# Weight buffers at two fixed remainders of 256 bytes in place of rotating ones, in a float32 decoder trunk

## The chip, the cores and the metric

The kernel runs on one core of one Trainium2 chip. The metric is the device time of one execution in microseconds (us), as a median over runs. Five engines work on a core: TensorE (PE; its weight loads are listed as PEld), VectorE (DVE), ScalarE (ACT), GpSimd (POOL) and SyncE (SP, which here issues the weight transfers). SBUF is the memory on the chip that they read; each of its 128 partitions holds its own bytes, and "address" below means the byte within a partition. PSUM holds what TensorE accumulates.

## The reference

The input is one sequence of 256 positions with 2048 features. Two layers follow. Each has a token mixer (layer 0 a gated linear recurrence, HGRN2; layer 1 a gated MLP with a spatial gate) and a gated feed-forward block with a causal convolution of width 3 and 5632 hidden features. Cut to what matters here:

```python
for layer in range(2):
    mixed = hgrn2_mixer(h, ...) if layer == 0 else chunked_gmlp(h, ...)
    h = layer_norm(ALPHA * h + mixed, ln1_g[layer], ln1_b[layer])
    up = h @ w_up                        # 2048 x 11264
    a, b = jnp.split(up, 2, axis=-1)
    a = causal_conv3(a) + conv_b
    h = layer_norm(ALPHA * h + (silu(a) * b) @ w_down, ln2_g[layer], ln2_b[layer])
# mixers: x @ w_in (2048 x 8192, or 2048 x 4096), the mixing itself, and @ w_out (2048 x 2048)
```

Everything is float32. Nearly all of the work is in the products with the weight matrices, and the activations are only 256 rows, so each weight is used for two tiles of 128 rows and then dropped.

## The kernel before

**Split operands.** A product of float32 numbers is made out of three products of shorter ones. Every operand is split into a high part (the value cast to the type fp32r) and a low part (the value less its high part). For activations, `X` holds the input of a mixer or of the feed-forward block and `Y` the input of the second product; both have the shape 128 x 16 x 2 x 256: 16 tiles k of 128 features, each with 256 high and then 256 low values (2048 bytes). The product is high x high + high x low + low x high.

**Weights.** They come in chunks of 512 features by 512 columns (`raw`, 128 x 4 x 512, 1 MB each). `fetch` (L73) issues the transfer on SP; `convert` (L83) makes the high part `whi` on ScalarE (L95) and the low part `wlo` on VectorE (L96), in two halves of 128 x 1024 each. The pool `wp` has three buffers for each of `raw`, `whi` and `wlo`, and chunks take them in turn. `chunk` keeps three chunks ahead of the one in use (`AHEAD = 3`). The order of the chunks is a list that `want` fills (`plan_hgrn`, `plan_gmlp`, `plan_ffn`). Six chunks of the program go to an extra pool `xp` instead.

**Two forms of product.** In `block_b` (L152) the weights are stationary and `X` streams through. For each k and each 128 columns j it issues two matmuls into the same PSUM tile: `rest` (L168) with the low weights loaded and 256 high values of `X` streamed, and `both` (L161) with the high weights loaded and all 512 values of `X` streamed. So long and short matmuls alternate, each with a weight load of 128 x 128 of its own, and a chunk has 16 of each. Where `halves` is set (one block for each feed-forward block), the long ones are in part cut into pieces of 256. In `block_a` (L112) the activations are stationary and 512 weight columns stream: three matmuls for each k and half t of the rows, L125 (high activations, high weights), L126 (high, low) and L127 (low, high); a chunk has 24. `staggered_pass` (L675 to L677) does the same for the last part of one product.

**Where the buffers lie.** Pools lay their tiles one behind the other, and tiles without a use (`pad0`, `pady`, `pad1`, `gap`) fill up between them. In the built program of before `X` starts at address 16,640, a multiple of 256; each of its tiles is a multiple of 1024 bytes, so every operand taken from it starts at remainder 0 of 256. `Y` starts at 49,600, remainder 192. `whi` and `wlo` have 16 floats (`SKEW`) more than they need, so their size is 8256 bytes, 64 more than a multiple of 256: the three `whi` start at remainders 0, 64 and 128 (126,720, 134,976, 143,232), and so do the three `wlo` (151,552, 159,808, 168,064), with `gap` between the two groups. A chunk's high and low buffers have the same remainder. The slices within a buffer are multiples of 512 bytes and don't change it. Chunk after chunk the buffers turn through the remainders in the order 0, 128, 64. The buffers of the extra pool start at remainder 224, both halves.

Of the kernel before, what the change touches and what calls it, by code (L numbers as in the profile page):

```python
# [9 lines left out]
F32R = mybir.dt.float32r  # L10
# [5 lines left out]
P = 128  # L16
# [9 lines left out]
NB = 512  # L26
CK = 4
# [2 lines left out]
FFN_GROUPS = (3, 4, 4)  # L30
AHEAD = 3
LINE = 256
PAD_Y = 192
PAD1 = 160
SKEW = 16
BLOCK = {1: 32, 4: 32, 16: 64}
XSEQ = ((0, 2, 4), (2, 2, 0), (4, 4, 1), (8, 4, 1), (12, 4, 0))
TURN_ACT = 3
# [2 lines left out]
class Trunk:  # L41
# [4 lines left out]
    def __init__(self, ctx, tc, a):  # L46
# [11 lines left out]
        self.X = cp.tile([P, NK, 2, S], F32R, name="X")  # L58
        cp.tile([P, PAD_Y], mybir.dt.uint8, name="pady")
        self.Y = cp.tile([P, NK, 2, S], F32R, name="Y")  # L60
        self.z = cp.tile([P, 2, D], F32, name="z")
        cp.tile([P, PAD1], mybir.dt.uint8, name="pad1")
        self.small = ent(tc.tile_pool(name="small", bufs=2))
# [19 lines left out]
    def convert(self, raw, extra, pieces=2):  # L83
        nc = self.nc
        pool = self.xp if extra else self.wp
        size = CK * NB + (0 if extra else SKEW)
        hi = pool.tile([P, size], F32R, tag="hi", name="whi")
        if not extra:
            pool.tile([P, LINE - 3 * 4 * SKEW], mybir.dt.uint8, tag="gap", name="gap", bufs=1)
        lo = pool.tile([P, size], F32R, tag="lo", name="wlo")  # L90
        hi, lo = (x[:, : CK * NB].rearrange("p (k n) -> p k n", k=CK) for x in (hi, lo))
        n = CK // pieces
        for i in range(0, CK, n):
            s = slice(i, i + n)
            nc.scalar.copy(hi[:, s, :], raw[:, s, :])  # L95
            self.last_lo = nc.vector.tensor_tensor(  # L96
                lo[:, s, :], raw[:, s, :], hi[:, s, :].bitcast(F32), ALU.subtract
            )
        self.ready.append((hi, lo))
# [800 lines left out]
```

## Time and profile before

| | before |
|---|---|
| median of 3 runs | 2296.53 us (2296.07 to 2297.42) |
| the profiled execution's own time | 2296.34 us |
| its span, from the first to the last instruction | 2294.6 us |
| mean granted TensorE clock | 0.998 |
| DMA | 430.14 MB, mean 187 GB/s |
| instructions in the span | 31751 |

Times in the profile come from the profiled execution. A row of a group of instructions gives line, engine, operation, output<-inputs with shapes, and behind the count (x) the busy time in us, the mean length of one in ns and the engine's idle time just before them. A matmul's record lasts from its start until its results are drained, and the next one starts long before that, so the lengths of records of neighbouring matmuls overlap, and a row's busy time counts overlapping time once. What a matmul costs in a dense stream is its spacing: the time from its start to the next one's start. A row of a stretch of time gives from:to in us, the length, TensorE's busy time with the number of instructions that touch the stretch, the granted clock, the DMA share and GB/s. A row of the timeline gives start in us, length in us, engine, line and operation.

### The profile page before, as it was taken

How to read it: one execution, taken by the hardware profiler on the slowest of the kernel's cores; microseconds unless marked ns; L12 is line 12 of the kernel's file. 1: busy time of each engine (PE TensorE's matmuls, PEld its weight loads, DVE VectorE, ACT ScalarE, POOL GpSimd, SP SyncE). 2: the span in 40 equal slices, each digit the busy share in tenths (PEclk: the TensorE clock that was granted, in tenths of full speed). 3: DMA queues.
4: the chain of work that ended last, by engine and by line, in shares of the span. 5: the costliest groups of instructions: out<-in, count | busy, mean ns of one | idle time of the engine just before them, and what ended most of it. 6: DMA issues, size and time to landing. Idle time of an engine off the chain costs nothing.

```text
span 2294.6 us, 31751 instructions
## 1 busy us (share of the span) xinstructions
PE 2272.9 (99%) x12781; PEld 1930.8 (84%) x12781; DVE 1473.2 (64%) x2327; ACT 1104.6 (48%) x1698; POOL 48.5 (2%) x102
## 2 busy tenths in 40 slices
PE   8999999999999999999999999999999999999998
PEld 7888888888888888888888888888888888888886
DVE  5767677667765665556656676566765666465655
ACT  5656565545443444344444554454543444344542
POOL 3000000000000000000000000000000000000000
PEclk9999999999999999999999999999999999999999
DMA  7454545645565555555555675655575555555563
GB/s 259 150 183 144 191 148 163 217 164 189 188 233 184 184 183 195 191 183 186 189 193 172 213 218 184 223 180 174 179 239 181 187 189 192 186 184 189 178 202 111
DMA packets 214052, 430.14 MB, mean 187 GB/s; under 512 B 7544, under 2 KB 8336, under 8 KB 213904
## 3 DMA queue, kind: packets, MB, share of 16 engines
q1 hardware_dynamic: 209536, 415.26, 54.4%
q0 software_dynamic: 4368, 12.85, 1.9%
q8 instruction: 100, 1.64, 0.3%
q14 instruction: 48, 0.39, 0.0%
HBM read 425.98 MB, written 2.10 MB: 187 GB/s over the span
## 4 chain that ended last, share of the span: by engine, by line
PE 97%; DVE 1%; ACT 1%; DMA 1%; SPq 0%; issue 0%; DVEq 0%; ACTq 0%
PE pb L161 38%; PE pb L168 20%; PE pa L125 12%; PE pa L127 12%; PE pa L126 12%; PE pl L552 1%; DMA z<-in_x_dram 1%; DVE wlo L96 0%; PE pt L307 0%; PE pg L754 0%; PE pa L677 0%; PE pa L675 0%; PE pa L676 0%; PE po L524 0%; PE pout L644 0%; ACT whi L95 0%
## 5 line engine op out<-in xcount | busy, mean ns | idle before, releaser
L96 DVE TENSOR_TENSOR wlo<-raw,whi 128x1024 fp32r<-128x1024 f32 (+1 forms) x786 | 930.0, 1218 | 704.9 <-ACT whi L95 696.6
L161 PE MATMUL pb<-X,whi 128*128 128x512 f32 (+1 forms) x3960 | 1344.3, 390 | 1.9 <-DVE X L319 1.9
L95 ACT CAST whi<-raw 128x1024 fp32r<-128x1024 f32 (+1 forms) x786 | 789.4, 1046 | 908.6 <-PE pb L161 426.0
L168 PE MATMUL pb<-X,wlo 128*128 128x256 f32 x3840 | 1055.8, 283 | 0.0
L161 PEld LDWEIGHTS pb<-X,whi 128*128 128x128 f32 x3960 | 725.6, 188 | 164.5 <-DVE X L319 2.4
L168 PEld LDWEIGHTS pb<-X,wlo 128*128 128x128 f32 x3840 | 714.8, 188 | 6.5
L125 PE MATMUL pa<-whi,Y 128*128 128x512 f32 x928 | 366.2, 395 | 0.0
L127 PE MATMUL pa<-whi,Y 128*128 128x512 f32 x928 | 365.8, 394 | 0.0
L126 PE MATMUL pa<-wlo,Y 128*128 128x512 f32 x928 | 365.0, 393 | 0.0
L127 PEld LDWEIGHTS pa<-whi,Y 128*128 128x128 f32 x928 | 174.6, 188 | 40.6
L126 PEld LDWEIGHTS pa<-wlo,Y 128*128 128x128 f32 x928 | 174.5, 188 | 40.5
L125 PEld LDWEIGHTS pa<-whi,Y 128*128 128x128 f32 x928 | 174.6, 188 | 39.0
L206 ACT COPY rest<-pb 128x256 f32<-128x256 f32 x240 | 87.8, 369 | 114.0 <-PE pb L161 105.8
L125 PE MATMUL pa<-whi,X 128*128 128x512 f32 x256 | 101.0, 394 | 0.0
L127 PE MATMUL pa<-whi,X 128*128 128x512 f32 x256 | 100.6, 393 | 0.0
L126 PE MATMUL pa<-wlo,X 128*128 128x512 f32 x256 | 100.3, 392 | 0.0
L805 DVE SCALAR_TENSOR_TENSOR act<-a,cols,act 128x254 f32<-128x254 f32 (+1 forms) x176 | 73.0, 475 | 0.0
L127 PEld LDWEIGHTS pa<-whi,X 128*128 128x128 f32 x256 | 48.1, 188 | 11.0
L126 PEld LDWEIGHTS pa<-wlo,X 128*128 128x128 f32 x256 | 48.1, 188 | 10.7
L125 PEld LDWEIGHTS pa<-whi,X 128*128 128x128 f32 x256 | 48.1, 188 | 10.3
L399 DVE TENSOR_TENSOR z<-z,pa 128x512 f32<-128x512 f32 x40 | 27.3, 683 | 36.1 <-PE pa L127 31.7
L809 ACT ACTIVATE act<-act 128x256 f32<-128x256 f32 x88 | 33.8, 415 | 7.8 <-DVE act L805 7.6
(164 smaller groups left out, 1030.2 us busy)
## 6 DMA issues: line engine op xcount, KB each, us to landing
raw<-in_ffn_w_up_dram SPq DMA_DIRECT2D x176, 1024.0 KB, 4.9
raw<-in_ffn_w_down_dram SPq DMA_DIRECT2D x88, 1024.0 KB, 4.9
raw<-in_hg_w_in_dram SPq DMA_DIRECT2D x63, 1024.0 KB, 5.1
raw<-in_sg_w_in_dram SPq DMA_DIRECT2D x32, 1024.0 KB, 5.3
raw<-in_hg_w_out_dram SPq DMA_DIRECT2D x16, 1024.0 KB, 4.9
raw<-in_sg_w_out_dram SPq DMA_DIRECT2D x16, 1024.0 KB, 4.9
g<-in_ln_g_dram POOLq DMA_DIRECT2D x16, 256.0 KB, 6.3
b<-in_ln_b_dram POOLq DMA_DIRECT2D x16, 256.0 KB, 8.5
```

The source lines that it names most:

```text
L95: nc.scalar.copy(hi[:, s, :], raw[:, s, :])
L96: self.last_lo = nc.vector.tensor_tensor(lo[:, s, :], raw[:, s, :], hi[:, s, :].bitcast(F32), ALU.subtract)
L125: nc.tensor.matmul(ps[t], xh, hi[:, kk, :], start=n[t] == 0, stop=False)
L126: nc.tensor.matmul(ps[t], xh, lo[:, kk, :], start=False, stop=False)
L127: nc.tensor.matmul(ps[t], xl, hi[:, kk, :], start=False, stop=last)
L161: nc.tensor.matmul(ps[j][:, :, s], ch[0][:, k % CK, c], act[:, k, :, s], start=start and k == 0, stop=k == last, skip_group_check=halves,)
L168: nc.tensor.matmul(ps[j][:, 1, :], ch[1][:, k % CK, c], act[:, k, 0, :], start=False, stop=False, skip_group_check=halves,)
L206: nc.scalar.copy(r, ps[:, 1, :])
L399: nc.vector.tensor_tensor(zz, zz, ps, ALU.add)
L552: nc.tensor.matmul(ps[n * j : n * j + n, th, :], K[:, own(th, n, j)], moving(th, j), start=True, stop=True, tile_position=(0, n * j),)
L805: nc.vector.scalar_tensor_tensor(cv[:, d:], x[:, : S - d], self.c(("cw", l, 2 - d), f), cv[:, d:], ALU.mult, ALU.add,)
L809: nc.scalar.activation(cv, cv, AF.Silu)
```

## The change

The skew of the weight buffers goes, and the pads get other sizes. All three high buffers start at a multiple of 256 bytes (126,720, 134,912, 143,104), as `X` does; all three low buffers start 128 beyond one (151,424, 159,616, 167,808), and `Y` too (49,536). What lies behind in SBUF moves down by 320 bytes, until the extra pools on the other side, which stay. No instruction is added or removed, and their order on every engine is the same.

```diff
-PAD_Y = 192
-PAD1 = 160
-SKEW = 16
+PAD_Y = 128
+PAD_LO = 128
+PAD1 = 224
...
         pool = self.xp if extra else self.wp
-        size = CK * NB + (0 if extra else SKEW)
-        hi = pool.tile([P, size], F32R, tag="hi", name="whi")
+        hi = pool.tile([P, CK, NB], F32R, tag="hi", name="whi")
         if not extra:
-            pool.tile([P, LINE - 3 * 4 * SKEW], mybir.dt.uint8, tag="gap", name="gap", bufs=1)
-        lo = pool.tile([P, size], F32R, tag="lo", name="wlo")
-        hi, lo = (x[:, : CK * NB].rearrange("p (k n) -> p k n", k=CK) for x in (hi, lo))
+            pool.tile([P, PAD_LO], mybir.dt.uint8, tag="gap", name="gap", bufs=1)
+        lo = pool.tile([P, CK, NB], F32R, tag="lo", name="wlo")
```

## Prediction

> **What bounds the kernel now.** I read the page first: the busy shares and the granted clock, then the chain that ended last.
>
> ```profile
> PE 2272.9 (99%) x12781; PEld 1930.8 (84%) x12781; DVE 1473.2 (64%) x2327; ACT 1104.6 (48%) x1698; POOL 48.5 (2%) x102
> PEclk9999999999999999999999999999999999999999
> PE 97%; DVE 1%; ACT 1%; DMA 1%; SPq 0%; issue 0%; DVEq 0%; ACTq 0%
> PE pb L161 38%; PE pb L168 20%; PE pa L125 12%; PE pa L127 12%; PE pa L126 12%; PE pl L552 1%; DMA z<-in_x_dram 1%; DVE wlo L96 0%; PE pt L307 0%; PE pg L754 0%; PE pa L677 0%; PE pa L675 0%; PE pa L676 0%; PE po L524 0%; PE pout L644 0%; ACT whi L95 0%
> ```
>
> TensorE is 97% of the chain, at full clock in every slice, and 94% is five lines: L161 and L168 of block_b, L125 to L127 of block_a. So the time is the number of matmuls times their spacing, from one's start to the next's, and a change of buffer addresses counts here if it moves that spacing. The number comes from the groups of instructions, shapes kept apart:
>
> ```profile
> L161 PE MATMUL pb<-X,whi 128*128 128x512 f32 x3720 | 1314.1, 397 | 0.0
> L168 PE MATMUL pb<-X,wlo 128*128 128x256 f32 x3840 | 1055.8, 283 | 0.0
> L125 PE MATMUL pa<-whi,Y 128*128 128x512 f32 x928 | 366.2, 395 | 0.0
> L125 PE MATMUL pa<-whi,X 128*128 128x512 f32 x256 | 101.0, 394 | 0.0
> ```
>
> That is 3720 pairs of a long and a short matmul in block_b, and in block_a 928 triples (L125, L126, L127) on Y and 256 on X. The 397 and 283 ns are lengths of records that overlap, not spacings.
>
> Next the timeline of one stretch, weight loads first, then matmuls: what runs beside what.
>
> ```profile
> 843.52 0.19 PEld L168 LDWEIGHTS pb<-X,wlo 128*128 128x128 f32 x1
> 843.75 0.19 PEld L161 LDWEIGHTS pb<-X,whi 128*128 128x128 f32 x1
> ```
>
> ```profile
> 843.52 0.39 PE L161 MATMUL pb<-X,whi 128*128 128x512 f32 x1
> 843.75 0.28 PE L168 MATMUL pb<-X,wlo 128*128 128x256 f32 x1
> 843.87 0.39 PE L161 MATMUL pb<-X,whi 128*128 128x512 f32 x1
> ```
>
> A load starts with the matmul before its own: while L161 streams X, the low weights of the next L168 are read; while L168 streams X, the high weights of the next L161. Each matmul thus has two readers in SBUF, the stream and the next load.
>
> Does the place of the two matter? The trace of before answers this, because its three buffers lie at remainders 0, 64 and 128 of 256 bytes. Below are stretches that I cut at the first matmul of a chunk (the program's buffers turn in the order 0, 128, 64). The first six are block_b chunks in that order, 32 matmuls each; then three chunks of block_a on Y in the order 0, 128, 64; three on X in the order 64, 0, 128, 24 matmuls each; the last is again a block_b chunk at remainder 0.
>
> ```profile
> 820.84:826.50 5.66, 5.66 (x34) 1.00 0.56 186
> 826.50:832.11 5.61, 5.61 (x33) 1.00 0.55 188
> 832.11:837.75 5.64, 5.64 (x34) 1.00 0.44 163
> 837.75:843.40 5.65, 5.65 (x33) 1.00 0.68 206
> 843.40:849.02 5.62, 5.62 (x34) 1.00 0.59 191
> 849.02:854.67 5.65, 5.65 (x34) 1.00 0.57 185
> 905.32:910.83 5.51, 5.51 (x26) 1.00 0.70 213
> 910.83:916.41 5.58, 5.58 (x25) 1.00 0.56 177
> 916.41:921.99 5.58, 5.58 (x26) 1.00 0.57 189
> 1294.67:1300.17 5.50, 5.50 (x25) 1.00 0.58 187
> 1300.17:1305.66 5.49, 5.49 (x25) 1.00 0.58 193
> 1305.66:1311.26 5.60, 5.60 (x26) 1.00 0.46 164
> 719.44:725.00 5.56, 5.56 (x34) 1.00 0.56 188
> ```
>
> The second column is the length. TensorE never idles, yet a chunk's length follows its buffer. Block_b, per pair: (5.66+5.65)/32 = 353.4 ns at remainder 0, 352.8 at 64, (5.61+5.62)/32 = 350.9 at 128; all six 33.83/96 = 352.4. In block_a, take the remainder of what is loaded (Y at 192, X at 0) less that of the streamed weights, modulo 256. On Y it is 192, 64, 128 for buffers 0, 128, 64 and costs 5.51, 5.58, 5.58 us; on X it is 192, 0, 128 for buffers 64, 0, 128 and costs 5.50, 5.49, 5.60. Equal differences cost nearly the same although the addresses differ: 192 gives 5.51 and 5.50, 128 gives 5.58 and 5.60. So the distance between the two readers is what counts.
>
> **The change, part by part.** No instruction, transfer or wait is added, removed or moved. X stays at remainder 0, the high buffers all come to 0, the low ones to 128, Y to 128. The six chunks in the extra pool keep remainder 224 for both halves.
>
> (a) Block_b. After, every long matmul runs beside a load from remainder 128 (low weights), as now only in the 128 buffers, and every short one beside a load from remainder 0, as now only in the 0 buffers. The groups of three neighbouring chunks, at 0, 128 and 64, give the two parts:
>
> ```profile
> L161 PE MATMUL pb<-X,whi 128*128 128x512 f32 x17 | 6.0, 398 | 0.0
> L168 PE MATMUL pb<-X,wlo 128*128 128x256 f32 x16 | 4.5, 281 | 0.0
> ```
>
> ```profile
> L161 PE MATMUL pb<-X,whi 128*128 128x512 f32 x17 | 6.0, 394 | 0.0
> L168 PE MATMUL pb<-X,wlo 128*128 128x256 f32 x17 | 4.8, 283 | 0.0
> ```
>
> ```profile
> L161 PE MATMUL pb<-X,whi 128*128 128x512 f32 x18 | 6.3, 397 | 0.0
> L168 PE MATMUL pb<-X,wlo 128*128 128x256 f32 x16 | 4.5, 281 | 0.0
> ```
>
> Records are longer than spacings by a nearly fixed amount: 398+281-353.4 = 325.6, 394+283-350.9 = 326.1, 397+281-352.8 = 325.2 for a pair, 325.6 on average. By parts the pair after is 394+281-325.6 = 349.4 ns. The parts are not free of each other, since a spacing depends on the one before it, so I go halfway to the nearest whole pattern measured, 350.9: 350.1 ns, 2.3 less than 352.4. Times 3720: -8.6 us. Bounds: the best pair seen at any remainder is 5.56/16 = 347.5 (-18.2 us); the worst mix of the parts is 398+283-325.6 = 355.4 (+11.2 us).
>
> (b) Block_a on Y. The differences become 128 for the two lines that stream high weights and 0 for the line that streams low: (2 x 5.58 + 5.49)/24 = 693.8 ns a triple, against (5.51+5.58+5.58)/24 = 694.6. Times 928: -0.8 us. Bounds: all at 5.49, -7.7; all at 5.60, +5.0. On X they become 0, 128, 0: (2 x 5.49 + 5.60)/24 = 690.8 against (5.50+5.49+5.60)/24 = 691.3, times 256: -0.1 us.
>
> (c) ScalarE and VectorE write the moved buffers and read them.
>
> ```profile
> L96 DVE TENSOR_TENSOR wlo<-raw,whi 128x1024 fp32r<-128x1024 f32 (+1 forms) x786 | 930.0, 1218 | 704.9 <-ACT whi L95 696.6
> L95 ACT CAST whi<-raw 128x1024 fp32r<-128x1024 f32 (+1 forms) x786 | 789.4, 1046 | 908.6 <-PE pb L161 426.0
> ```
>
> Both stand idle about as long as they work there (908.6/786 = 1.2 us before a cast, mostly until TensorE gives a buffer back, and 0.9 us before a subtraction), so a few per cent either way costs nothing. Were that cover gone, 1% would be 10 ns on each of 786 casts, 8 us. The small tiles of the mixers all shift by the same 320 bytes, and their matmuls are about 1% of the chain: 0.
>
> Sum: -8.6-0.8-0.1 = -9.5 us on the profiled execution's 2296.34 us (span 2294.6): 2286.8. The median of the runs is 0.2 above that execution, so 2287.0.
>
> One rule speaks against any effect. The Trainium skill, SBUF — State Buffer, Who interferes with whom, says that PE never waits on anyone and gives it two separate read ports; by that the sum would be 0 and the time 2296.5. The chunks above, 5.61 to 5.66 us for equal work, do not agree with it.
>
> **The rivals.** *No change.* Each placing is a pattern of waits that the two readers settle into, and the new one may settle at about the mean of the old three. For it: all whole patterns lie within 1.5 ns of 352.4, apart from the odd 347.5. Against: then the parts would have to work together worse than in any buffer now. Time 2296.5, chance 0.18; the page's rule ends here too.
>
> *Slower: the other half counts.* Within a chunk now the running and the loading weights have one remainder, so the rows above can't tell which sets the spacing. If it is the running matmul's own weights, the long matmul keeps the 398 of high weights at 0 and the short one takes the 283 of low weights at 128: +11.2 us, with (b) 2306.8. The one place where they differ is the seam between chunks: the last long matmul of a buffer at 0, while the next chunk's low weights at 128 load. Two seams in the timeline:
>
> ```profile
> 826.26 0.40 PE L161 MATMUL pb<-X,whi 128*128 128x512 f32 x1
> 826.50 0.28 PE L168 MATMUL pb<-X,wlo 128*128 128x256 f32 x1
> ...
> 860.08 0.39 PE L161 MATMUL pb<-X,whi 128*128 128x512 f32 x1
> 860.30 0.28 PE L168 MATMUL pb<-X,wlo 128*128 128x256 f32 x1
> ```
>
> The first takes 0.24 us (for it), the second 0.22 (against). With a short one at 281 less half of 325.6, 118 ns, it decides from the point where the long one averages over 352.4-118 = 234 ns. Against it stands block_a, where equal loading distances cost the same. Chance 0.12.
>
> *Faster still.* Block_b settles into the 347.5 ns pattern: -18.2-0.9 gives 2277.4. For it: by parts 349.4 is close. Against: that pattern is one chunk after a switch from block_a, while the later chunks at 0 went back to 353.4. Chance 0.15. That the change doesn't do what it says has no room: sizes of 8192 bytes and pads of 128 and 224 fix the remainders.
>
> **How the numbers follow.** The forecast, 2287.0, has 0.55; faster still 0.15; no change 0.18; slower 0.12. The range reaches from a little below "faster still" (less a quarter of the lower bound of (b), 1.9, and the 1.4 by which the three runs differ: 2274) over "no change" to half of the slower rival's price (2296.5+5.6-0.9 = 2301), leaving out about 0.15. A measurement of this kernel tells about 0.2%, 4.6 us, from no change. Faster by more than that: 0.55+0.15 = 0.70; within: 0.18; slower: 0.12.
>
> **What would show it.** Right: every block_b chunk has one length, near 5.60 us, with L161 near 394 and L168 near 281 in its groups; block_a on Y near 5.55 us in every chunk; casts and subtractions still 1.05 and 1.22 us. Wrong: block_b chunks at 5.64 (no change), at 5.68 with L168 at 283 (slower), or any new idle time of TensorE.

## The result, and the profile after

The changed kernel takes 2281.96 us (median of 6 runs, 2281.66 to 2282.49), the kernel before 2296.39 us (6 runs, 2296.07 to 2297.42). The ratio is 0.9937, 95% interval 0.9924 to 0.995: 14.4 us faster, of which the profiled executions show 14.0 (spans 2294.6 and 2280.6 us, granted clock 0.998 in both). The forecast was 2287.0, 9.5 us faster.

All names keep their meaning, but line numbers after the change are two lower: L159 and L166 are `both` and `rest` of block_b (L161 and L168 before), L123 to L125 the three lines of block_a (L125 to L127), L93 and L94 the cast and the subtraction. First the page of the kernel after: busy shares, the start of the chain that ended last, and the two engines that make the weights.

```profile
PE 2258.8 (99%) x12781; PEld 1925.7 (84%) x12781; DVE 1473.4 (65%) x2327; ACT 1105.4 (48%) x1698; POOL 48.5 (2%) x102
...
PE 97%; DVE 2%; ACT 1%; DMA 0%; issue 0%; SPq 0%; DVEq 0%; ACTq 0%
...
L94 DVE TENSOR_TENSOR wlo<-raw,whi 128x1024 fp32r<-128x1024 f32 (+1 forms) x786 | 930.6, 1219 | 693.3 <-ACT whi L93 684.9
...
L93 ACT CAST whi<-raw 128x1024 fp32r<-128x1024 f32 (+1 forms) x786 | 790.2, 1047 | 894.8 <-PE pb L159 418.7
```

TensorE is still the whole chain, with the same 12781 instructions. Casts and subtractions take 1047 and 1219 ns (1046 and 1218 before), so the moved addresses mean nothing to ScalarE and VectorE. TensorE's busy time fell by 14.1 us (2272.9 to 2258.8), the whole gain. The groups of matmuls, shapes kept apart, say on which lines:

```profile
L159 PE MATMUL pb<-X,whi 128*128 128x512 f32 x3720 | 1304.6, 395 | 0.0
L166 PE MATMUL pb<-X,wlo 128*128 128x256 f32 x3840 | 1049.7, 281 | 0.0
L123 PE MATMUL pa<-whi,Y 128*128 128x512 f32 x928 | 365.4, 394 | 0.0
...
L123 PE MATMUL pa<-whi,X 128*128 128x512 f32 x256 | 101.8, 398 | 0.0
```

The long matmul of block_b went from 397 to 395 ns and the short one from 283 to 281. In block_a the first line became 1 ns shorter on Y (394 for 395) and 4 longer on X (398 for 394). Those are lengths that overlap; spacings come from stretches cut at the first matmul of a chunk. Three block_b chunks, two of block_a on Y, one on X:

```profile
817.28:822.88 5.60, 5.60 (x33) 1.00 0.55 182
822.88:828.48 5.60, 5.60 (x34) 1.00 0.58 189
828.48:834.06 5.58, 5.58 (x33) 1.00 0.44 166
895.62:901.11 5.49, 5.49 (x25) 1.00 0.45 175
901.11:906.61 5.50, 5.50 (x26) 1.00 0.68 213
66.13:71.73 5.60, 5.60 (x25) 1.00 0.78 219
```

The three lengths by buffer (5.66, 5.61, 5.65) are gone. To compare kernels I cut three longer stretches at the same places of the program in each: 16 chunks of block_a on Y (128 triples), the 32 chunks of block_b behind them (512 pairs), and 6 chunks of block_a on X in layer 1 (48 triples). Before:

```profile
899.75:988.66 88.91, 88.91 (x386) 1.00 0.57 190
988.66:1168.97 180.31, 180.31 (x1026) 1.00 0.57 187
1278.08:1311.26 33.18, 33.18 (x146) 1.00 0.68 221
```

And after:

```profile
895.62:983.51 87.89, 87.89 (x385) 1.00 0.57 192
983.51:1162.56 179.05, 179.05 (x1025) 1.00 0.57 188
1270.84:1304.43 33.59, 33.59 (x145) 1.00 0.66 218
```

Block_b: 180.31/512 = 352.2 to 179.05/512 = 349.7 ns a pair, times 3720: -9.2 us. Block_a on Y: 694.6 to 686.6 ns a triple, times 928: -7.4 us. Block_a on X: 691.3 to 699.8 ns, times 256: +2.2 us. Together -14.4 us: the three stretches account for the result.

### The profile page after: what moved, and what is told of

It reads as the page before. It is cut to its first block, busy times and chain, and to the rows that moved or that the text cites. A ratio compares the mean times of both kernels' runs of the same rounds, so it can differ in the third digit from the quotient of the medians.

```text
span 2280.6 us, 31751 instructions
## 1 busy us (share of the span) xinstructions
PE 2258.8 (99%) x12781; PEld 1925.7 (84%) x12781; DVE 1473.4 (65%) x2327; ACT 1105.4 (48%) x1698; POOL 48.5 (2%) x102
## 4 chain that ended last, share of the span: by engine, by line
PE 97%; DVE 2%; ACT 1%; DMA 0%; issue 0%; SPq 0%; DVEq 0%; ACTq 0%
PE pb L159 38%; PE pb L166 20%; PE pa L123 12%; PE pa L125 12%; PE pa L124 12%; DVE wlo L94 1%; PE pl L550 1%; PE pt L305 1%; ACT whi L93 0%; PE pg L752 0%; PE pa L673 0%; PE pa L675 0%; PE pa L674 0%; DMA z<-in_x_dram 0%; PE po L522 0%; PE pout L642 0%
## 5 line engine op out<-in xcount | busy, mean ns | idle before, releaser
L94 DVE TENSOR_TENSOR wlo<-raw,whi 128x1024 fp32r<-128x1024 f32 (+1 forms) x786 | 930.6, 1219 | 693.3 <-ACT whi L93 684.9
L159 PE MATMUL pb<-X,whi 128*128 128x512 f32 (+1 forms) x3960 | 1335.1, 388 | 1.9 <-DVE X L317 1.9
L93 ACT CAST whi<-raw 128x1024 fp32r<-128x1024 f32 (+1 forms) x786 | 790.2, 1047 | 894.8 <-PE pb L159 418.7
L166 PE MATMUL pb<-X,wlo 128*128 128x256 f32 x3840 | 1049.7, 281 | 0.0
L159 PEld LDWEIGHTS pb<-X,whi 128*128 128x128 f32 x3960 | 725.0, 188 | 160.1 <-DVE X L317 2.3
L166 PEld LDWEIGHTS pb<-X,wlo 128*128 128x128 f32 x3840 | 715.7, 189 | 6.1
L123 PE MATMUL pa<-whi,Y 128*128 128x512 f32 x928 | 365.4, 394 | 0.0
L125 PE MATMUL pa<-whi,Y 128*128 128x512 f32 x928 | 363.5, 392 | 0.0
L125 PEld LDWEIGHTS pa<-whi,Y 128*128 128x128 f32 x928 | 173.9, 187 | 40.4
L123 PEld LDWEIGHTS pa<-whi,Y 128*128 128x128 f32 x928 | 174.9, 188 | 35.6
L123 PE MATMUL pa<-whi,X 128*128 128x512 f32 x256 | 101.8, 398 | 0.0
L125 PE MATMUL pa<-whi,X 128*128 128x512 f32 x256 | 100.6, 393 | 0.0
L125 PEld LDWEIGHTS pa<-whi,X 128*128 128x128 f32 x256 | 48.1, 188 | 11.8
L123 PEld LDWEIGHTS pa<-whi,X 128*128 128x128 f32 x256 | 48.1, 188 | 11.4
```

Source lines behind the costliest of these rows:

```text
L94: self.last_lo = nc.vector.tensor_tensor(lo[:, s, :], raw[:, s, :], hi[:, s, :].bitcast(F32), ALU.subtract)
L123: nc.tensor.matmul(ps[t], xh, hi[:, kk, :], start=n[t] == 0, stop=False)
L125: nc.tensor.matmul(ps[t], xl, hi[:, kk, :], start=False, stop=last)
L159: nc.tensor.matmul(ps[j][:, :, s], ch[0][:, k % CK, c], act[:, k, :, s], start=start and k == 0, stop=k == last, skip_group_check=halves,)
L166: nc.tensor.matmul(ps[j][:, 1, :], ch[1][:, k % CK, c], act[:, k, 0, :], start=False, stop=False, skip_group_check=halves,)
```

## The experiments

Two theories stood at first. **Theory A**, the prediction's: a matmul's spacing depends on the distance, modulo 256, between the weights or activations that are being loaded and the data that stream. **Theory B**, the slower rival's: it depends on the running matmul's own operands. Every kernel below differs from the one before only in where its buffers lie; the instructions and their order are the same. The edit of each is given by the constants for the pads, in place of the skew of before: `PAD_X` ahead of X, `PAD_Y` ahead of Y, `PAD_H` ahead of the three high weight buffers, `PAD_L` between the high and the low ones; PAD1 behind Y takes up the difference. In the table, hi and lo are the remainders of the high and low weight buffers, and Y, block_b and X the three stretches above in us.

| kernel | X, Y | hi, lo | time, us | ratio to before (95%) | Y | block_b | X |
|---|---|---|---|---|---|---|---|
| before | 0, 192 | (0,0), (64,64), (128,128) | 2296.39 | | 88.91 | 180.31 | 33.18 |
| after | 0, 128 | 0, 128 | 2281.96 | 0.9937 (0.9924 to 0.995) | 87.89 | 179.05 | 33.59 |
| swap | 0, 128 | 128, 0 | 2299.07 | 1.001 (1.0 to 1.0019) | 89.59 | 180.16 | 32.96 |
| shift64 | 64, 192 | 64, 192 | 2282.43 | 0.994 (0.9925 to 0.9955) | 87.90 | 179.04 | 33.28 |
| weights_only | 0, 192 | 0, 128 | 2285.36 | 0.9951 (0.9936 to 0.9966) | 88.46 | 179.04 | 32.96 |
| y_only | 0, 128 | as before | 2296.59 | 1.0 (0.9991 to 1.001) | 88.89 | 180.31 | 33.17 |
| y0 | 0, 0 | 0, 128 | 2293.06 | 0.9985 (0.9976 to 0.9994) | 89.59 | 179.04 | 33.60 |
| same0 | 0, 192 | 0, 0 | 2286.28 | 0.9958 (0.9944 to 0.9972) | 87.90 | 180.46 | 32.65 |
| uni64 | 0, 64 | 64, 0 | 2281.06 | 0.9932 (0.9919 to 0.9944) | 87.93 | 179.03 | 33.60 |
| uni192 | 0, 64 | 192, 0 | 2261.15 | 0.9845 (0.9832 to 0.9859) | 88.75 | 174.91 | 33.76 |

**swap.** The halves of the weights change places.

```diff
-SKEW = 16
+PAD_X, PAD_Y = 128, 128
+PAD_H, PAD_L = 128, 128
```

> The halves change places: high buffers at remainder 128, low ones at 0, Y at 128, X at 0. Theory A (the load that runs beside a matmul sets its spacing): long matmuls run beside loads from 0 (record 398 ns), short ones beside loads from 128 (283 ns): pair 355 ns, chunk 5.69 us, +5 ns on 3720 pairs against the changed kernel, +20 us; block_a on Y gets the differences 0, 128, 0 that block_a on X has in the changed kernel (5.60 us a chunk, +12 us), block_a on X gets 128, 0, 128 (5.49 us, -3 us): about 2311 us. Theory B (the weights already loaded set it): pair 349 ns or 350, and with the same block_a 2291 us.

The stretches of swap, in the order Y, block_b, X:

```profile
900.03:989.62 89.59, 89.59 (x385) 1.00 0.56 188
989.62:1169.78 180.16, 180.16 (x1025) 1.00 0.56 187
1279.43:1312.39 32.96, 32.96 (x146) 1.00 0.67 223
```

Against (load remainder less stream remainder for the high, then the low weights) after has (128, 0) on Y and (0, 128) on X; swap has the reverse, and the lengths trade places: 699.9 ns a triple on Y, as after on X (699.8), and 32.96/48 = 686.7 on X, as after on Y (686.6). That is the distance that Theory A goes by. Theory B asks for the same here, since in block_a the activations in use and those that are being loaded lie at one remainder; only block_b tells the two apart. There a pair takes 351.9 ns, 2.2 above after, so the order of the halves matters in the direction of A; but the size fits neither A's sum of parts (355.4) nor B's (349.4). So the distance holds, and adding parts does not.

**shift64.** Everything of after 64 bytes further on.

```diff
-SKEW = 16
+PAD_X, PAD_Y = 192, 128
+PAD_H, PAD_L = 64, 128
```

> The changed kernel with X, Y and all weight buffers moved by 64 bytes (X and high at 64, Y and low at 192), so that all distances stay. If distances alone count: 2282 us within 2, chunks 5.60 us (block_b), 5.49 (block_a on Y), 5.60 (block_a on X). If starting at a multiple of 256 is what helps: towards the 2296 of before.

```profile
895.61:983.51 87.90, 87.90 (x386) 1.00 0.56 192
983.51:1162.55 179.04, 179.04 (x1025) 1.00 0.57 188
1270.87:1304.15 33.28, 33.28 (x145) 1.00 0.67 221
```

The first two are those of after to 0.01 us, though none of these buffers starts at a multiple of 128 any more. The multiples that the change speaks of are not what counts; the distances between operands are. The third, on X in layer 1, missed the expectation: 693.3 ns a triple where after has 699.8, on the same distances. On X in layer 0 both kernels have 5.59 and 5.60 us a chunk. So a distance does not fix one length everywhere; the runs below come back to this.

**weights_only and y_only.** The two halves of the change, each alone: the weight buffers with Y left at 192, and Y at 128 with the weight buffers left turning.

```diff
-SKEW = 16                 # weights_only
+PAD_X, PAD_Y = 128, 192
+PAD_H, PAD_L = 0, 128
...
-PAD_Y = 192               # y_only
+PAD_Y = 128
```

> The weight buffers of the changed kernel, with Y left at remainder 192 as before. Distances: block_b chunks 5.60 us as in the changed kernel; block_a on Y gets the differences 192, 64, 192, which by parts from the chunks of before is (2 x 5.505 + 5.588)/3 = 5.53 us a chunk, +4.6 us: 2286.5 us; block_a on X 5.60 us. If the placing of Y does nothing: 2282 us.

> The kernel before with Y at remainder 128 instead of 192, weight buffers still turning. Distances: block_a on Y takes 5.58, 5.58 and 5.49 us for buffers at 0, 64 and 128 (differences 128, 64, 0), 0.02 us a chunk less than before on average: 2295.5 to 2296.5 us, and block_b as before (5.66, 5.65, 5.61). If the placing of Y by itself brings what block_a gained: 2289 us.

The Y stretch of weights_only, then three chunks of block_a on Y in y_only, with the buffers at 64, 0, 128 and so at differences 64, 128, 0:

```profile
896.53:984.99 88.46, 88.46 (x386) 1.00 0.57 191
```

```profile
1455.39:1460.99 5.60, 5.60 (x25) 1.00 0.91 261
1460.99:1466.56 5.57, 5.57 (x25) 1.00 1.02 398
1466.56:1472.05 5.49, 5.49 (x25) 1.00 0.84 300
```

The weights alone give 11.0 of the 14.4 us, Y alone nothing: its three buffers average 694.2 ns a triple for 694.6. Y's move is worth 3.4 us only beside the new weights (691.1 to 686.6 ns times 928 is -4.2). The gain is not the sum of the two edits. And X, whose placing in weights_only is that of after, took 32.96 us in its stretch for 33.59: 686.7 ns a triple in place of 699.8, on equal differences. In layer 0 the two kernels agree on X, at 5.59 and 5.60 us a chunk (699.8 ns).

**y0.** After, with Y at remainder 0: the differences on Y become those that X has in after.

```diff
-SKEW = 16
+PAD_X, PAD_Y = 128, 0
+PAD_H, PAD_L = 0, 128
```

> The change with Y at remainder 0 in place of 128, all else as after. Block_a on Y then has the differences 0, 128, 0, those of X in after. Theory A by parts, as the prediction had it: a triple is the sum of its lines, (2 x 5.49 + 5.60)/3 = 5.53 us a chunk, and 928 triples cost 3.8 us more than in after: 2286. Theory C: the parts of a triple don't add, the sequence of differences as a whole counts: 5.60 us as on X in after, 13.4 ns x 928 = 12.4 us more: 2294. Block_b 5.60 us in both.

```profile
898.34:987.93 89.59, 89.59 (x385) 1.00 0.56 188
```

699.9 ns a triple: Theory C, not the sum of the parts. Over the whole run 2293.06 us, 1 below C's 2294, because some chunks ran at 5.55 us in place of 5.60, with the same addresses.

**The scans.** Each buffer gets a placing of its own, three to a kernel; X is at 0 and Y at 128.

```diff
+PADS = (0, 0, 64, 0, 128, 64)   # scan1, in front of the three high, then the three low buffers
...
+        hi, lo = (
+            pool.tile([P, CK, NB], F32R, tag=x if extra else f"{x}{i}", name="w" + x, bufs=1)
+            for x in ("hi", "lo")
+        )
```

> Each of the three buffers gets its own placing (high, low): (0, 64), (0, 192), (64, 0); X at 0, Y at 128. If the parts add, a block_b chunk is 16 times the long record for the low remainder plus the short record for the high one less 325.6 ns: 5.64 us for (0, 64) and 5.65 for (64, 0); for a low half at 192 the trace of before has nothing. Block_a by parts: on Y 5.58, 5.56, 5.59 us, on X 5.50, 5.52, 5.50. If the waits of neighbouring matmuls mix, as the 5.63 us of the swapped kernel instead of 5.69 suggests: any value between 5.55 and 5.67, in no order by parts.

> Placings (high, low) (64, 128), (64, 192), (128, 64); X at 0, Y at 128. By parts block_b 5.59 us for (64, 128) and 5.67 for (128, 64); block_a on Y 5.56, 5.56, 5.52 us, on X 5.53, 5.53, 5.56. If the waits mix: block_b between 5.55 and 5.67 in no order by parts.

> Placings (high, low) (128, 192), (192, 0), (192, 64); X at 0, Y at 128. For high weights at 192 the trace of before has nothing, so block_b is open between 5.55 and 5.67 us. Block_a by parts on Y 5.49, 5.53, 5.53 us, on X 5.58, 5.56, 5.56.

> Placings (high, low) (0, 128), (192, 128), (192, 192); X at 0, Y at 128. (0, 128) is the changed kernel's: 5.60 us in block_b, 5.49 on Y and 5.60 on X, if a chunk's length depends on its own buffer and not on its neighbours'. (192, 192) keeps both distances equal as in before: 5.60 to 5.66. Block_a by parts for the last two on Y 5.50 and 5.50 us, on X 5.59 and 5.59.

One run each: scan1 (0,64), (0,192), (64,0) 2281.31 us; scan2 (64,128), (64,192), (128,64) 2291.42; scan3 (128,192), (192,0), (192,64) 2281.30; scan4 (0,128), (192,128), (192,192) 2281.14; before on the same chip 2296.39. Three neighbouring block_b chunks of scan1, at (64,0), (0,64), (0,192):

```profile
1110.97:1116.41 5.44, 5.44 (x34) 1.00 0.57 184
1116.41:1121.96 5.55, 5.55 (x33) 1.00 0.47 175
1121.96:1127.58 5.62, 5.62 (x33) 1.00 0.71 210
```

5.44 us is 340 ns a pair, shorter than anything in before or after. But a placing did not keep one length: (64,0) took 5.44 in 32 of 68 chunks of the scan and 5.58 to 5.60 in 31, and (192,0) in scan3 5.44 to 5.48 in 45 of 71 and 5.60 in 19. (0,128), the change's own, ran at 5.55 in scan4 in 60 of 72 chunks, where after has 5.60. What runs before a chunk matters too.

**uni64 and uni192.** The two placings that had shown 5.44 us, in all three buffers.

```diff
-SKEW = 16
+PAD_X, PAD_Y = 128, 64
+PAD_H, PAD_L = 64, 192   # uni64
+PAD_H, PAD_L = 192, 64   # uni192
```

> High weights at remainder 64 in all three buffers, low weights at 0, X at 0, Y at 64. In the first scan the chunks of block_b at (64, 0) took 5.44 us 32 times of 68, and 5.58 to 5.60 else. If the placing alone sets the rhythm, every block_b chunk takes one length: at 5.44 us (340 ns a pair, 10 less than after) the time is 2282.0 - 37 = 2245 us, at 5.60 it is 2282. If a chunk takes over the rhythm that the one ahead of it leaves, the mean of the scan, 5.51 us, is not what comes out, since the neighbours now are of the same kind: one of the two lengths then holds from chunk to chunk and changes only after other work. Block_a on Y has differences 0 and 64 (5.52 to 5.53 us in the second scan, +1 to +4 against 5.49 in after), on X 192 and 0 (5.54, against 5.60 in after): +3 us together at the most.

> High weights at remainder 192 in all three buffers, low weights at 0, X at 0, Y at 64. In the third scan the chunks of block_b at (192, 0) took 5.44 us 24 times of 71, 5.47 to 5.48 21 times and 5.60 23 times. One length throughout if the placing alone sets the rhythm: 5.44 us gives 2245 us, 5.475 gives 2253, 5.60 gives 2282. Block_a on Y has differences 128 and 64 (5.55 us in the first scan, against 5.49 in after: +7 us), on X 64 and 0 (5.60 in the second scan, as after). So 2252, 2260 or 2289.

uni192 beats both kernels: 2261.15 us, 20.8 below after, at ratio 0.9845. In it the block_b stretch begins with four chunks at one length and goes on at another (chunks 3 to 6 of that stretch):

```profile
986.11:991.71 5.60, 5.60 (x33) 1.00 0.56 190
991.71:997.32 5.61, 5.61 (x34) 1.00 0.54 182
997.32:1002.79 5.47, 5.47 (x33) 1.00 0.45 172
1002.79:1008.23 5.44, 5.44 (x33) 1.00 0.66 210
```

The timeline of uni192 around 997.3 us shows the switch; the second column is the length of a record, the starts are what to read:

```profile
996.73 0.40 PE L161 MATMUL pb<-X,whi 128*128 128x512 f32 x1
996.96 0.28 PE L168 MATMUL pb<-X,wlo 128*128 128x256 f32 x1
997.08 0.64 PE L161 MATMUL pb<-X,whi 128*128 128x512 f32 x2
997.56 0.28 PE L168 MATMUL pb<-X,wlo 128*128 128x256 f32 x1
997.68 0.39 PE L161 MATMUL pb<-X,whi 128*128 128x512 f32 x1
997.90 0.28 PE L168 MATMUL pb<-X,wlo 128*128 128x256 f32 x1
998.02 0.39 PE L161 MATMUL pb<-X,whi 128*128 128x512 f32 x1
998.25 0.28 PE L168 MATMUL pb<-X,wlo 128*128 128x256 f32 x1
998.36 0.39 PE L161 MATMUL pb<-X,whi 128*128 128x512 f32 x1
```

Ahead of it pairs start 0.35 us apart (996.73, 997.08), behind it 0.34 (997.68, 998.02, 998.36), on the same two lines and the same remainders. Between them stand two long matmuls in a row (x2). That is where four chunks, one set of output columns, are done: for k = 0 `one` issues `both` ahead of `rest`, for every other k `rest` first. This break in the alternation comes every four chunks, and a rhythm changes there or stays. uni64 kept the longer rhythm through every break of its stretch (179.03 us); elsewhere in the same run it changed to the shorter one at a break and back at the next, four chunks on (the third and the fourth of them, 5.44 and 5.43 us, are left out):

```profile
1574.38:1579.98 5.60, 5.60 (x34) 1.00 0.58 186
1579.98:1585.48 5.50, 5.50 (x34) 1.00 0.45 172
1585.48:1590.92 5.44, 5.44 (x34) 1.00 0.73 210
...
1601.79:1607.37 5.58, 5.58 (x33) 1.00 0.47 174
```

The expectation that a placing has one length fell; that a rhythm holds until other work breaks it held. In each of the eight kernels with one placing for all weight buffers, behind the program's first set, none of the 106 steps from the second chunk of a set to the third, or from the third to the fourth, changed the length by more than 0.02 us. So, as far as these runs go, the placing decides which rhythms are possible and the history which one runs.

**same0.** All weights at remainder 0, Y at 192: one placing instead of three, but without the offset between the halves.

```diff
-SKEW = 16
+PAD_X, PAD_Y = 128, 192
+PAD_H, PAD_L = 0, 0
```

> One part of the change alone: all weight buffers at one remainder, but the low half not apart from the high one (both at 0, X at 0, Y at 192 as before). Theory D, the gain is in holding one placing and not turning through three: block_b gets shorter than the 5.64 us that is the mean of before, down to the 5.56 us that a buffer at 0 showed once after other work, and the time is 2296.4 - 0.08 x 232 - 7.3 - 1.2 = 2269 us. Theory E, each placing has the spacing that its buffer showed in before, and the gain of the change is in the offset of 128 between the halves: block_b 5.655 us in every chunk, 3720 x (353.4 - 352.4) = +3.7 us, block_a on Y at difference 192 in every chunk 686.7 ns a triple, 928 x -7.9 = -7.3 us, block_a on X at difference 0 5.49 us, -1.2 us: 2291.6 us.

```profile
2010.55:2016.09 5.54, 5.54 (x33) 1.00 0.57 190
2016.09:2021.64 5.55, 5.55 (x34) 1.00 0.58 188
2021.64:2027.19 5.55, 5.55 (x34) 1.00 0.57 193
2027.19:2032.83 5.64, 5.64 (x33) 1.00 0.43 164
```

It came out between D's 2269 and E's 2291.6 us, nearer E. Block_b ran at 5.64 to 5.66 us in 163 of 212 whole chunks (those without other work in between), but at 5.55 in some 40: 12 of them the second to fourth chunks behind a switch from block_a on Y, until the break, the others in the mixers and at the start of the feed-forward blocks. The stretch is 180.46 us, no better than before, so in block_b the gain (179.05) comes from the offset of the low half and not from holding one placing. That is shown for a placing at 0; both halves at 128 in every buffer, the shortest of the three of before, was not run. On Y it is different: same0 has the 87.90 us of after with another placing, so there the gain comes from dropping the two slower buffers. uni64 makes the same point the other way round: other differences on Y, again 87.93.

## Why the prediction was right in direction and short in size

**(a) Block_b: right.** Forecast 350.1 ns a pair and -8.6 us, measured 349.7 and -9.2. Of 212 whole chunks 197 took 5.58 to 5.60 us, as the prediction asked, and 12 took 5.55, with L159 at 395 and L166 at 281. Going halfway from the sum of the parts (349.4) to a whole pattern (350.9) landed well, but swap shows that this was partly luck: there the same sum says 355.4 and the chip 351.9.

**(b) Block_a: the step that failed.** The words were "(2 x 5.58 + 5.49)/24 = 693.8 ns a triple" for Y, "-0.8 us", and "(2 x 5.49 + 5.60)/24 = 690.8" for X, "-0.1 us". Measured: 686.6 and -7.4 us, 699.8 and +2.2 us. Both are mis-sized for one reason: a chunk length measured with all three differences equal was shared out line by line, and the lines don't add. A triple with differences 128, 0, 128 ran faster than two thirds of 128 and one third of 0 would make it, one with 0, 128, 0 as slowly as three lines at 128 would (5.60/8 = 700). swap and y0 give the same two numbers with other buffers. Even so a triple has no single price: X in layer 1 took 686.7 in weights_only and 693.3 in shift64 on the differences that cost 699.8 in after. The Y term lay inside its bound (-7.7); for X no bound was given, and the all-5.60 one would have held it. The two terms make -5.2 us where the forecast had -0.9; with the 0.6 of (a) they account for the whole 4.9 us between the forecast sum (-9.5) and that of the three stretches (-14.4).

**(c) ScalarE and VectorE: right**, 1 ns apart, and no new idle time of TensorE.

**The rivals.** *No change* fell: the four kernels with after's distances between X and the weights all have block_b at 179.04 or 179.05 us. *Slower: the other half counts* fell: it asked for 355.4 ns a pair in after, and got 349.7; in swap, where the same idea asks for 349.4, the pair took 351.9. What the prediction held against it in block_a did not count: there both theories see the same distance. *Faster still* fell for after, but what it rested on is real: the odd 347.5 ns pattern of before is a second rhythm of that placing, seen again in same0, where it ends at the break. The prediction saw that it did not last and could not say why. That a placing has several rhythms was on no list, and by it uni192 got 20.8 us more than the change.

The rule that the prediction set against itself, the Trainium skill's SBUF — State Buffer, Who interferes with whom, by which PE waits on nobody and reads through two separate ports, is not borne out here for TensorE against itself: between swap and uni192 lie 37.9 us, 1.6%, with the same instructions and other addresses. ScalarE and VectorE, which write and read the same buffers, are not the cause. In the block_b stretch of after, pairs with ScalarE busy for over 95% of their time (199 of them) took 349.5 ns and pairs with it busy for under 5% (212) 350.1; by VectorE's time it is 349.6 (283) and 349.9 (156). That it is the load and the stream that wait for each other, and not the weights in use, rests on block_b in after and swap; which part of the chip makes them wait, no run here shows.

What stays open: which rhythm a placing falls into. The block_b stretch has one length to 0.01 us in after, shift64, weights_only and y0, so it is not chance there, but none of the theories foretold 5.44 at (192,0), nor why uni64 mostly misses it.

## What to carry to other kernels

Where one engine streams without idling, cut its timeline at equal pieces of work and look whether their lengths depend on the buffer; if they do, the addresses of what is loaded and what streams, relative to each other, are a knob. Don't price a new placing by adding up lines from old ones: measure whole patterns, in the order in which the instructions run, and allow for more than one length each. A kernel that holds one placing everywhere is also easier to tune, since a trial measures one placing and not a mix of three: the best of five uniform placings of the weights was worth 35 us.

## What the runs showed of the hardware that was not expected

- The spacings are regular and come in steps. Pairs: 340.0 ns (5.44/16, uni192), 346.7 (16.64/48, the three chunks of same0 up to 2027.19), 353.4 (before, buffer at 0). Triples: 680.2 (32.65/48, same0 on X), 686.6 (after on Y), 693.4 (88.75/128, uni192 on Y), 699.9 (y0 on Y). Neighbours differ by 6.4 to 6.8 ns; some stretches, like the 349.7 of after, lie between two.
- The same instructions on the same remainders run at 350 or 340 ns a pair in one execution (uni192), and kept to the one or the other from break to break.
- The Trainium skill's TensorE: Matmul & The Clock Gate, Back-to-back issue gap, gives N/2.4 + 2.5 ns as the gap of an isolated matmul at full clock, and says that this counts too much for long ones in a stream; worked out for a pair of 512 and 256 columns it is 325 ns, an estimate. The best rhythm here, 340 ns, is 15 above it, so no run here shows such a saving.
